# Gathered rows in a PEER layer: later picks behind every third block, and stores of a tile two pairs of blocks later

## The chip, the cores and the metric

One core of a Trainium2 chip runs the kernel. The metric is the device time of one execution in microseconds (us), the median of three runs; smaller is better. A profile comes from one further execution, which has its own time.

## The reference

Two decoder layers on 256 tokens of width 1024: a mixer (attention, then a convolution module), and after each mixer a PEER expert layer. The expert layer is what the change is about:

```python
u = expert_u[ec]                      # ec: 8 heads x 16 chosen experts of 16384 for each token
act = jax.nn.gelu(jnp.einsum('cd,chkd->chk', xc, u))
w = gc.astype(xc.dtype) * act
return jnp.einsum('chk,chkd->cd', w, expert_v[ec])
```

## The kernel before, in words

The kernel doesn't gather the rows of `expert_u`. In `peer` (L589) it goes through all 16384 experts in 128 blocks of 128, two blocks (a pair, `pi`) at a time: `s1_pair` (L162) multiplies a block of `u` with all 256 tokens, GELU is taken, and the result is multiplied by the gates of the tokens for these experts. Gates are mostly zero. They are made on TensorE in steps of 8 tokens while the pairs run (`gate_bank`), from pair 22 on; the first 128 tokens (a tile) have all their gates at pair 37, the second at pair 53 (`done`, the number of steps made, times `TB` = 8 tokens).

The second half of the layer multiplies the gated activations with the rows of `expert_v`. The last 32 blocks (`i` from 96 to 127) are taken as they lie: **the plain blocks**, 32 of them, each 12 matmuls of 128x512 (two tiles of tokens, two halves of the width, three terms of a split into high and low parts). Of the first 96 blocks only experts that some token uses are multiplied. For these, a table `expert` says which rows make up 84 new blocks of 128 rows, **the picked blocks**: 81 in the list `mixed` (42 that both tiles use, 12 matmuls each, and 39 that one tile uses, 6 matmuls; they alternate, both tiles first, and the last three are for both) and 3 in `ends`. The activations of the first 96 blocks are therefore written to a table `rows` in HBM, token columns by expert rows, with one DMA for 8 blocks and one tile (`send`, L627, on SP's queue).

Each picked block needs two indirect DMAs, both issued on POOL's queue:

- **a gather** (`picked`, L719): 128 rows of `expert_v`, 128x1024 f32, into one of four buffers `raw`. ACT casts it to `hi` (L122), DVE makes `lo` (L128), which frees the buffer, and TensorE multiplies (L146 to L148).
- **a pick** (`rows_of`, L726): the same 128 rows of `rows`, 128x256 f32, into one of 64 slots of `wr`. ACT casts it to `wh` (L731, in `row_parts`), DVE makes `wl` (L732). Slots are used again from the 65th pick on.

`pick` (L617) paces the picks: each has a dependence on the cast `wh` of the block that is being multiplied (`behind`). Once all 24 stores of `rows` are written into the program, two picks come behind each plain block, up to 64; then one comes behind each picked block until all 84 are made. A queue runs in order: a gather that stands behind a waiting pick waits too.

The order of instructions on each engine is not the program's. A scheduler places them by its own simulated times, so what the change moves is read from the built programs. At block `k` = 60 of `mixed` there is a conditional part (L697) that isn't taken with these inputs. Layer 0 and layer 1 of the PEER part are the same, except that layer 0's also prepares the convolution (`conv_prep`).

Of the kernel before, what the change touches and what calls it, by code (L numbers as in the profile page):

```python
# [15 lines left out]
P = 128  # L16
D = 1024
KC = D // P
T = 256
NT = T // P  # L20
# [17 lines left out]
HI = NK // 2  # L38
NC = 4 * TK + (TK - 4) * 4
TB = 8  # L40
# [5 lines left out]
NI = NK - ND  # L46
# [18 lines left out]
class Trunk:  # L65
# [523 lines left out]
    def peer(self, l, acc):  # L589
        nc, I = self.nc, self.I  # L590
        new = lambda: self.store_tile("st").rearrange("p (i t) -> p i t", t=T)
        st = [new()]
        sl = lambda i, n=2: st[i // HI][:, i % HI:i % HI + n, :]

        g = self.gain(2 * l + 1, st[0][:, HI - D // T:, :].rearrange("p i t -> p (i t)"))
        xT = self.norm_T(g, acc)
        U = I["u"][l]
        self.route_open(l)
        for h in range(PH):
            ps = self.s1_pair([I["wpq"][l, 2 * h], I["wpq"][l, 2 * h + 1]], xT, POOL_Q, h == 0)  # L600
            qT = self.qT[h % 2]
            nc.scalar.copy(qT, ps)
            self.route_scores(l, h, qT)
        route = self.route_steps()
        steps = 2 * (PH + 13)
        nb = T // TB
        done = 0
        rows = self.tc.dram_tile([NI * NK, T], F32, name=self.nm("rows"))
        out = rows.rearrange("(i j) t -> j i t", j=NK)
        sent = [0] * NT  # L610
        order = None
        mixed, ends = self.plan()
        turns = [b for _, b in mixed + ends]
        slot = lambda n: room[:, n % HI, :]
        picked = 0

        def pick(n, behind, most=HI):  # L617

            nonlocal picked
            for _ in range(min(n, min(most, len(turns)) - picked)):  # L620
                ins = self.rows_of(rows, turns[picked], slot(picked))
                self.tc.add_manual_dep(ins.ins, behind.ins.name,
                                       mybir.DependencyInfo(mybir.DependencyClass.Sync, mybir.DependencyReason.DATA),
                                       reason="pace")
                picked += 1

        def send(n, most):  # L627

            for t in range(NT):
                while most and done * TB >= (t + 1) * P and min(sent[t] + 8, NI) <= n and sent[t] < n:  # L630
                    i = sent[t]
                    m = min(8, n - i)
                    to = NT if t == 0 and sent[1] == i and done * TB >= T else t + 1
                    ts = slice(t * P, to * P)
                    nc.sync.dma_start(out[:, i:i + m, ts], sl(i, m)[:, :, ts])
                    for k in range(t, to):
                        sent[k] = i + m
                    most -= 1

        for pi in range(NK // 2):  # L640
            if pi == G0:
                for _ in route:
                    pass
                st.append(new())
                self.gates_open()
                self.one_hots(0)
                self.one_hots(1)
            due = min(max(0, pi + 1 - G0) * (nb // 2) // (G1 - G0), nb // 2) * 2
            todo = list(range(done, due))
            done = due  # L650
            if pi == G1:
                order = self.order_steps()

            def between(j):
                if j == 0:
                    for b in todo:
                        for q in range(TB // TQ):
                            self.gate_bank(b, q, 2 * pi, st)
                    if order is not None:
                        for _ in range(2):  # L660
                            next(order, None)

            ps = self.s1_pair([U[2 * pi], U[2 * pi + 1]], xT, between=between)
            for b in todo:
                if b + 2 < nb:
                    self.one_hots(b + 2)
            self.expert_rows(ps, sl(2 * pi), done * TB)
            if pi < G0:
                for _ in range((pi + 1) * steps // G0 - pi * steps // G0):
                    next(route, None)  # L670
            send(min(2 * pi - 2, NI), 1)
        for _ in order:
            pass

        room = self.store_tile("wr").rearrange("p (n t) -> p n t", t=T)
        acc = self.s2_open()
        self.begun = [[False] * 2 for _ in range(NT)]
        last = len(ends)
        for i in range(NI, NK):
            behind = self.expert_products(acc, self.weights(I["v%d" % l][i]), sl(i, 1)[:, 0, :], range(NT))  # L680
            send(NI, 1)
            if sent == [NI] * NT:
                pick(2, behind)
        prep = None
        for k, (ts, b) in enumerate(mixed):
            if k == 2:
                if l + 1 == DEPTH:
                    self.g_out = self.gain(2 * DEPTH, self.store_tile("g")[:, 0:D])
                else:
                    prep = self.conv_prep(l + 1)  # L690
            if prep is not None:
                next(prep, None)
            self.expert_products(acc, self.picked(l, b), slot(k), ts,
                                 0 in ts and not any(0 in v for v, _ in mixed[k + 1:]))
            pick(1, self.first_part, k + 1 + HI)
            if k == 3 * len(mixed) // 4:
                with self.tc.If(self.rest_needed > 0, preferred_fallthrough_block=False):  # L697
                    for b2 in range(NB):
                        ts2 = [t for t, (lo, hi) in enumerate(((0, A_END), (B_BEG, B_END))) if not lo <= b2 < hi]
                        if ts2:  # L700
                            w = self.wc.tile([P, T], F32, tag="wh", name=self.nm("wr"))
                            self.rows_of(rows, b2, w)
                            self.expert_products(acc, self.picked(l, b2), w, ts2)
        for _ in prep or ():
            pass
        ends = [(self.picked(l, b), self.row_parts(slot(len(mixed) + n), ts)) for n, (ts, b) in enumerate(ends)]
        prev = None
        for h in range(2):
            for n, (w, a) in enumerate(ends):
                mms = self.s2_mm(acc, w, a, 1, h, False, n == last - 1)  # L710
                if prev is not None:
                    self.after(mms[0], prev)
                prev = mms[-1]
        return acc
# [463 lines left out]
```

## Time and profile before

| | us |
|---|---|
| median of 3 runs | 1796.91 |
| lowest and highest | 1796.32, 1797.37 |
| the profiled execution's own time | 1814.46 |
| its span in the trace | 1812.7 |

| engine | busy us | share |
|---|---|---|
| TensorE, matmuls | 1735.5 | 96% |
| VectorE (DVE) | 1308.4 | 72% |
| ScalarE (ACT) | 913.4 | 50% |
| GpSimd (POOL) | 522.9 | 29% |

The span is the time between the first and the last instruction that the trace has. Matmuls are pipelined, so their busy time is no measure of how close TensorE is to its peak; the starts of the matmuls and of the work that feeds them say more. An indirect DMA shows on POOL with the time that POOL takes to issue it, not with the time of the transfer. The average over the whole span hides the stages: the two stretches of picked blocks, some 200 us each, have limits of their own.

### The profile page before, as it was taken

What the parts mean: (1) busy time and instruction counts of PE and PEld (TensorE: products, weight loads), DVE (VectorE), ACT (ScalarE), POOL (GpSimd) and SP (SyncE); (2) the same over time, 40 slices, a digit from 0 to 9 for tenths busy, and PEclk for the clock granted to TensorE, in tenths of its full rate; (3) what the DMA queues carried; (4) which work ended last, traced back from release to release, by engine and by line L of the source; (5) the groups of instructions that cost most, each with busy time, mean ns of one, the idle gap of its engine ahead of it and who ended that gap; (6) DMA issues with size and microseconds to landing.
All of it is one profiled execution on the core that took longest, in us unless ns stands there. A gap on an engine that the chain in (4) does not pass through costs nothing. (4 is left out here: it accounts for less than half of the span.)

```text
span 1812.7 us, 32893 instructions
## 1 busy us (share of the span) xinstructions
PE 1735.5 (96%) x12606; PEld 1580.6 (87%) x12606; DVE 1308.4 (72%) x2720; ACT 913.4 (50%) x1515; POOL 522.9 (29%) x447
## 2 busy tenths in 40 slices
PE   7999999999998998898999899999999999988988
PEld 6879999999998986677798799999999998866766
DVE  4667994787988655576788589947879886545656
ACT  4653455544443444676654534555444434445655
POOL 1304000000000577654376340000000006777543
PEclk9999999999999999899999899999999999999999
DMA  7435555447467777676742355554385677767765
GB/s 268 140 123 192 175 178 191 151 152 249 164 197 245 244 271 236 216 253 217 251 141 81 111 187 171 185 185 152 141 256 166 204 247 252 271 211 237 248 213 196
DMA packets 146284, 361.13 MB, mean 199 GB/s; under 512 B 13248, under 2 KB 64704, under 8 KB 146112
## 3 DMA queue, kind: packets, MB, share of 16 engines
q1 hardware_dynamic: 113856, 248.76, 40.6%
q0 software_dynamic: 32256, 110.12, 18.7%
q8 instruction: 103, 1.69, 0.4%
q14 instruction: 69, 0.57, 0.1%
HBM read 332.61 MB, written 26.21 MB: 198 GB/s over the span
## 5 line engine op out<-in xcount | busy, mean ns | idle before, releaser
L122 ACT CAST hi<-raw 128x1024 fp32r<-128x1024 f32 x576 | 602.9, 1048 | 611.5 <-PE ps_h L162 389.8
L128 DVE TENSOR_TENSOR lo<-raw,hi 128x1024 fp32r<-128x1024 f32 x530 | 647.2, 1222 | 315.7 <-ACT hi L122 287.1
L162 PE MATMUL ps_h<-xh,hi 128*128 128x256 f32 x2560 | 730.2, 286 | 2.3 <-ACT hi L122 2.3
L162 PE MATMUL ps_h<-xh,lo 128*128 128x256 f32 x2560 | 723.9, 284 | 4.7 <-DVE lo L128 4.6
L162 PE MATMUL ps_h<-xo,hi 128*128 128x256 f32 x2560 | 718.7, 284 | 0.0
L162 PEld LDWEIGHTS ps_h<-xh,lo 128*128 128x128 f32 x2560 | 491.7, 192 | 6.0 <-DVE lo L128 5.9
L162 PEld LDWEIGHTS ps_h<-xh,hi 128*128 128x128 f32 x2560 | 492.3, 192 | 4.6 <-ACT hi L122 2.5
L162 PEld LDWEIGHTS ps_h<-xo,hi 128*128 128x128 f32 x2560 | 488.5, 192 | 0.2
L726 POOL DMA_INDIRECT wr<-rows,expert x168 | 190.9, 1136 | 906.7 <-ACT ps_h L1078 843.2
L147 PE MATMUL acc<-lo,wh 128*128 128x512 f32 x760 | 305.3, 402 | 4.2 <-DVE lo L128 2.1
L148 PE MATMUL acc<-hi,wl 128*128 128x512 f32 x760 | 301.1, 396 | 0.0
L146 PE MATMUL acc<-hi,wh 128*128 128x512 f32 x760 | 222.9, 402 | 33.1 <-ACT hi L122 21.8
L719 POOL DMA_INDIRECT raw<-in_v_dram,expert x168 | 185.9, 1107 | 144.1 <-DVE wl L732 57.2
L146 PEld LDWEIGHTS acc<-hi,wh 128*128 128x128 f32 x760 | 143.0, 192 | 76.1 <-ACT hi L122 32.6
L147 PEld LDWEIGHTS acc<-lo,wh 128*128 128x128 f32 x760 | 145.8, 192 | 49.1 <-DVE lo L128 13.0
L148 PEld LDWEIGHTS acc<-hi,wl 128*128 128x128 f32 x760 | 145.8, 192 | 30.0
L128 POOL TENSOR_TENSOR lo<-raw,hi 128x1024 fp32r<-128x1024 f32 x46 | 109.5, 2385 | 137.5 <-ACT hi L122 124.2
L731 ACT CAST wh<-wr 128x256 fp32r<-128x256 f32 (+1 forms) x168 | 58.3, 349 | 62.1 <-PE acc L147 30.5
L1049 PE MATMUL ps_g<-oh 128*128 128x128 f16 x1024 | 87.0, 219 | 0.0
L1053 PE MATMUL uses<-oh 128*128 128x96 f16 x512 | 83.1, 204 | 0.0
L1066 DVE SCALAR_TENSOR_TENSOR st<-ps_g,st 128x256 f32<-128x256 f32 (+5 forms) x216 | 64.7, 334 | 24.1 <-PE ps_g L1049 24.1
L732 DVE TENSOR_TENSOR wl<-wr,wh 128x256 fp32r<-128x256 f32 (+1 forms) x168 | 59.1, 353 | 29.3 <-ACT wh L731 20.8
(210 smaller groups left out, 1509.4 us busy)
## 6 DMA issues: line engine op xcount, KB each, us to landing
raw<-in_u_dram SPq DMA_DIRECT2D x256, 512.0 KB
raw<-in_v_dram SPq DMA_DIRECT2D x64, 512.0 KB
rows<-st SPq DMA_DIRECT2D x48, 512.0 KB
raw<-in_wpq_dram SPq DMA_DIRECT2D x32, 512.0 KB
raw<-in_pw_dram SPq DMA_DIRECT2D x24, 512.0 KB
raw<-in_wqk_dram SPq DMA_DIRECT2D x16, 512.0 KB
raw<-in_wv_dram SPq DMA_DIRECT2D x8, 512.0 KB
raw<-in_wo_dram SPq DMA_DIRECT2D x8, 512.0 KB
```

The costliest lines, as they stand in the source:

```text
L122: ins = [nc.scalar.copy(hi, raw)]
L128: ins.append(eng.tensor_tensor(lo, raw, hi.bitcast(F32), op=ALU.subtract))
L146: return [mm(ps, wh, xh, start=first, stop=False), mm(ps, wh, xo, start=False, stop=False), mm(ps, wo, xh, start=False, stop=last)]
L147: mm(ps, wh, xo, start=False, stop=False),
L148: mm(ps, wo, xh, start=False, stop=last)]
L162: mm = self.nc.tensor.matmul(ps[:, j, :], w[:, c * P:(c + 1) * P], x[:, c, :], start=n == 0, stop=n == len(terms) - 1)
L719: self.nc.gpsimd.indirect_dma_start(raw, None, self.I["v%d" % l].rearrange("i j d -> (i j) d"), bass.IndirectOffsetOnAxis(ap=self.expert[: ...
L726: return self.nc.gpsimd.indirect_dma_start(w, None, rows, at)
L732: self.nc.vector.tensor_tensor(lo[:, cs], w[:, cs], hi[:, cs].bitcast(F32), op=ALU.subtract)
L1049: mm = nc.tensor.matmul(ps[:, t, :], self.oh[:, b % 2, 0, tp, :, e], self.oh[:, b % 2, 1 + k, tp, :, e], start=k == 0, stop=k == 1)
L1053: use = nc.tensor.matmul(self.uses[:, tok // P, :], self.oh[:, b % 2, 0, tp, :, e], self.oh[:, b % 2, 1, tp, 0:NI, e], start=tok == 0, sto ...
L1066: nc.vector.scalar_tensor_tensor(v, ps[:, :, lo:lo + m].rearrange("p t i -> p i t"), 1.0 / GS, v, op0=ALU.mult, op1=ALU.mult)
```

## The change

Two edits. In the loop over `mixed`, a pick comes behind every third block (`k % 3 == 0`) and not behind every block. And `send` goes by the gates that were done two pairs of blocks earlier (`past[-3]`), so that the program writes the stores of a tile two pairs later than it did.

```diff
         done = 0
+        past = [0] * 3
...
         def send(n, most):
+            summed = past[-3]
             for t in range(NT):
-                while most and done * TB >= (t + 1) * P and min(sent[t] + 8, NI) <= n and sent[t] < n:
+                while most and summed * TB >= (t + 1) * P and min(sent[t] + 8, NI) <= n and sent[t] < n:
...
-                    to = NT if t == 0 and sent[1] == i and done * TB >= T else t + 1
+                    to = NT if t == 0 and sent[1] == i and summed * TB >= T else t + 1
...
+            past.append(done)
             send(min(2 * pi - 2, NI), 1)
...
-            pick(1, self.first_part, k + 1 + HI)
+            if k % 3 == 0:
+                pick(1, self.first_part, k + 1 + HI)
```

Lines behind L630 have other numbers in the changed kernel: its gathers are L726, its picks L733, its casts `wh` L738.

SP's, ACT's and DVE's instructions stand in the same order in both programs, the 48 stores of `rows` among them; in TensorE's, two matmuls of one picked block have changed places. POOL's order has changed. The stores of the last groups of 8 blocks move from the plain block 96 to the plain blocks 96 to 98 in the program, so the two picks a block begin at plain block 98 and not at 96: 60 picks are made behind plain blocks, not 64, and 24 are left for the picked blocks, not 20. With one behind every third block, the last is made behind block 69.

POOL, layer 0, where the picked blocks begin (`wr` are picks, `raw` gathers, `conv` a memset of the convolution's buffers). Before:

```order
L726 DMA wr_7625<-rows_2057,expert 128x256 x60
L719 DMA raw_8399<-in_v_dram,expert 128x1024
L726 DMA wr_7625<-rows_2057,expert 128x256 x2
L719 DMA raw_8422<-in_v_dram,expert 128x1024
L726 DMA wr_7625<-rows_2057,expert 128x256 x2
L435 MEMSET conv_8439 128x1
L436 MEMSET conv_8439 128x8x30
L719 DMA raw_8444<-in_v_dram,expert 128x1024
L726 DMA wr_7625<-rows_2057,expert 128x256
L719 DMA raw_8468<-in_v_dram,expert 128x1024
L726 DMA wr_7625<-rows_2057,expert 128x256
L719 DMA raw_8486<-in_v_dram,expert 128x1024
```

The same place with the change:

```order
L733 DMA wr_7623<-rows_2057,expert 128x256 x56
L726 DMA raw_8395<-in_v_dram,expert 128x1024
L733 DMA wr_7623<-rows_2057,expert 128x256 x2
L726 DMA raw_8418<-in_v_dram,expert 128x1024
L733 DMA wr_7623<-rows_2057,expert 128x256 x2
L435 MEMSET conv_8434 128x1
L436 MEMSET conv_8434 128x8x30
L726 DMA raw_8439<-in_v_dram,expert 128x1024
L733 DMA wr_7623<-rows_2057,expert 128x256
L726 DMA raw_8462<-in_v_dram,expert 128x1024
L726 DMA raw_8480<-in_v_dram,expert 128x1024
L733 DMA wr_7623<-rows_2057,expert 128x256
```

Before, a pick stands between any two gathers from the third on, until the 23rd; now there is one for about three gathers, the last behind the 71st. In layer 1 two to four gathers stand between picks.

POOL, layer 0, where the gathers reach the conditional part. Before:

```order
L719 DMA raw_9582<-in_v_dram,expert 128x1024
L719 DMA raw_9605<-in_v_dram,expert 128x1024
L719 DMA raw_9622<-in_v_dram,expert 128x1024
L883 TENSOR_LOAD fitu
L697 COMPARE_AND_BRANCH
```

With the change:

```order
L726 DMA raw_9578<-in_v_dram,expert 128x1024
L733 DMA wr_7623<-rows_2057,expert 128x256
L726 DMA raw_9601<-in_v_dram,expert 128x1024
L726 DMA raw_9618<-in_v_dram,expert 128x1024
L733 DMA wr_7623<-rows_2057,expert 128x256
L890 TENSOR_LOAD fitu
L704 COMPARE_AND_BRANCH
```

Picks now stand among the gathers here, and one right ahead of the load that the branch goes by.

ACT in the changed program, the same order as before, in the middle of layer 0's picked blocks (`hi` is the cast of a gather, `wh` that of a pick's slot; `wh_9096` belongs to the block of `raw_9090`):

```order
L122 CAST hi_9051<-raw_9049 128x1024
L738 CAST wh_9096<-wr_7623 128x256
L444 ACTIVATE conv_8434<-ident,conv_8434 128x128
L122 CAST hi_9074<-raw_9072 128x1024
L738 CAST wh_9119<-wr_7623 128x128
L444 ACTIVATE conv_8434<-ident,conv_8434 128x128
L122 CAST hi_9092<-raw_9090 128x1024
```

Nothing moved here. The cast `wh` of a block stands right behind the cast `hi` of the block two earlier.

## Rows read from the trace of the kernel before

**Rows 1.** The page: span, and busy time, share of the span and instructions of each engine.
```profile
span 1812.7 us, 32893 instructions
...
PE 1735.5 (96%) x12606; PEld 1580.6 (87%) x12606; DVE 1308.4 (72%) x2720; ACT 913.4 (50%) x1515; POOL 522.9 (29%) x447
```

**Rows 2.** Stretches: us, busy of each engine, PE clock, DMA share, GB/s.
```profile
609.00:690.00 81.00, 79.50 (x347) 64.52 (x346) 46.74 (x58) 39.20 (x58) 58.80 (x55) 1.00 0.78 263
690.00:759.00 69.00, 59.28 (x218) 44.59 (x217) 32.51 (x45) 34.99 (x65) 51.50 (x49) 0.88 0.71 220
759.00:838.00 79.00, 78.38 (x334) 61.32 (x333) 55.65 (x75) 59.20 (x113) 43.21 (x39) 1.00 0.77 252
1592.00:1660.00 68.00, 57.73 (x225) 41.52 (x224) 34.90 (x47) 29.64 (x46) 53.68 (x47) 0.97 0.72 224
```

**Rows 3.** POOL in order of time, layer 0: start, duration, instruction, [idle before].
```profile
689.83 1.16 POOL L719 DMA_INDIRECT raw<-in_v_dram,expert  x1 [0.30 <-issue]
...
698.97 0.95 POOL L719 DMA_INDIRECT raw<-in_v_dram,expert  x1 [0.16 <-DMA wr<-rows,expert]
700.22 1.38 POOL L726 DMA_INDIRECT wr<-rows,expert  x1 [0.30 <-issue]
701.91 0.94 POOL L719 DMA_INDIRECT raw<-in_v_dram,expert  x1 [0.30 <-issue]
703.16 0.94 POOL L726 DMA_INDIRECT wr<-rows,expert  x1 [0.30 <-issue]
704.40 0.94 POOL L719 DMA_INDIRECT raw<-in_v_dram,expert  x1 [0.30 <-issue]
...
757.13 1.22 POOL L726 DMA_INDIRECT wr<-rows,expert  x1 [0.30 <-issue]
758.65 0.94 POOL L719 DMA_INDIRECT raw<-in_v_dram,expert  x1 [0.30 <-issue]
...
765.73 0.94 POOL L719 DMA_INDIRECT raw<-in_v_dram,expert  x1 [1.85 <-DMA raw<-in_v_dram,expert]
...
835.44 0.94 POOL L719 DMA_INDIRECT raw<-in_v_dram,expert  x1 [1.56 <-DVE wl L732]
837.41 0.94 POOL L719 DMA_INDIRECT raw<-in_v_dram,expert  x1 [1.03 <-DVE lo L128]
845.88 0.94 POOL L719 DMA_INDIRECT raw<-in_v_dram,expert  x1 [7.53 <-DVEq L697]
```

**Rows 4.** POOL in order of time, layer 1, three gathers.
```profile
1604.71 0.94 POOL L719 DMA_INDIRECT raw<-in_v_dram,expert  x1 [0.31 <-issue]
...
1666.06 0.93 POOL L719 DMA_INDIRECT raw<-in_v_dram,expert  x1 [1.46 <-DVE lo L128]
...
1736.90 0.94 POOL L719 DMA_INDIRECT raw<-in_v_dram,expert  x1 [1.88 <-DVE wl L732]
```

**Rows 5.** POOL groups, 701.9 to 759, then 765 to 838: busy, mean ns | idle.
```profile
L726 POOL DMA_INDIRECT wr<-rows,expert x19 | 21.8, 1147 | 8.6 <-issue 5.2 <-DVE wl L732 3.1 <-DVE lo L128 0.3
L719 POOL DMA_INDIRECT raw<-in_v_dram,expert x20 | 20.7, 1034 | 6.9 <-issue 5.5 <-DVE wl L732 1.4
...
L719 POOL DMA_INDIRECT raw<-in_v_dram,expert x35 | 40.1, 1146 | 34.4 <-DVE wl L732 16.0 <-DVE lo L128 11.7 <-DMA raw<-in_v_dram,expert 3.9
```

**Rows 6.** Waits, 690 to 760, then 765 to 838: total us, times, longest.
```profile
ACT hi L122 <- DMA raw<-in_v_dram,expert: 17.2, 11, 3.3
...
POOL raw L719 <- DVE wl L732: 16.0, 13, 1.7
ACT hi L122 <- DMA raw<-in_v_dram,expert: 12.1, 17, 1.2
```

**Rows 7.** ACT, then POOL, in order of time, plain blocks of layer 0.
```profile
614.14 0.41 ACT L731 CAST wh<-st 128x256 fp32r<-128x256 f32 x1 [1.36 <-PE acc L147]
...
616.86 0.41 ACT L731 CAST wh<-st 128x256 fp32r<-128x256 f32 x1 [1.36 <-PE acc L147]
...
612.09 0.94 POOL L726 DMA_INDIRECT wr<-rows,expert  x1 [1.82 <-ACT wh L731]
```

## The prediction

> **What bounds the kernel now.** The page first, for the size: a span of 1812.7 us, TensorE's matmuls busy in 96% of it, POOL in 29% [rows 1]. By these shares a change to POOL's queue is worth nothing. But they are averages, so I read the stages next. In the plain blocks (609 to 690) and in the picked blocks from 759 on, TensorE is busy nearly throughout. In the first picked blocks it isn't: 59.28 of 69 us in layer 0 and 57.73 of 68 in layer 1, where the DMA engines move 220 to 224 GB/s against 263 in the plain blocks and 252 later [rows 2]. So data come late there, though the DMA engines have room.
>
> Third, POOL in order of time. From the fourth gather at 701.91 to the 23rd at 758.65, picks and gathers take turns, and nearly each starts 0.30 us behind the one before, released by nothing but "issue" [rows 3]. A pick takes 1147 ns and a gather 1034 ns of POOL in that stretch, so a block needs at least 1.147 + 1.034 + 2 x 0.30 = 2.78 us. The rows give (758.65 - 701.91) / 19 = 2.99 us. Picks end at 757.13. From the 27th gather (765.73) to the 60th (835.44) a block takes 69.71 / 33 = 2.11 us [rows 3], in layer 1 (1736.90 - 1666.06) / 33 = 2.15 [rows 4]. Mean: 2.13 us. POOL is idle for 34.4 us before those 35 gathers and waits for DVE, that is, for a free buffer [rows 5]. Fourth, the waits agree: ACT waits 17.2 us for gathered data in the early stretch, 11 times, 3.3 us at worst; later 12.1 us, 17 times and 1.2 at worst, and POOL's waits for DVE come first [rows 6].
>
> So **POOL's issuing sets the pace of the first 23 picked blocks of each layer**. What is then the floor of TensorE? A plain block of 12 matmuls takes 616.86 - 614.14 = 2.72 us [rows 7]. Picked blocks have 12 or 6, 9 in the mean, so 2.04 us. At 2.13 the gather-only stretch is near it.
>
> **The stores, two pairs later.** SP's order is the same in both programs, so this edit moves no store. What it does: 60 picks are made behind plain blocks, not 64. The four that drop out are the first ones, for blocks 96 and 97. Would that bring the first gather forward? No: the ninth pick, at 612.09, waited 1.82 us for ACT's cast [rows 7], so the queue has no backlog there to lose, and from then on the picks wait for the same casts as before. I cost it at nothing and keep the first four gathers (689.83 to 701.91) as they are, with the third one late at 698.97 [rows 3]. If that cover is gone, four issues of 1.45 us a layer come off.
>
> **The picks behind every third block.** Three gathers and a pick take POOL 3 x (1.034 + 0.30) + 1.147 + 0.30 = 5.45 us, 1.82 a block [rows 5]. That is below 2.13, so POOL no longer sets the pace. The new pace is 2.13 plus x, where x is a third of what one pick costs in a stretch that was free of picks. The trace has no such stretch, so I bound a pick:
> - from below by nothing. POOL has 34.4 / 35 - 0.30 = 0.68 us a block to spare there, 2.05 in three blocks, more than the pick's 1.45.
> - by data: a pick moves 128x256 numbers, a quarter of a gather's 128x1024. Were the DMA engines the limit, it would cost a quarter of 2.13, 0.53 us. Their share is 0.77 [rows 2], so they are not quite that.
> - from above by the whole of POOL's 1.45 us, if it always stands just ahead of a gather whose buffer is free.
>
> I take 0.25 us, about half of the data price, since POOL's spare time covers its issue: x = 0.08, a pace of 2.21.
>
> Does a pick now hold up the gathers behind it? It waits for the cast `wh` of its block, and ACT makes this right behind the cast `hi` of the block two earlier. The gather ahead of the pick in the queue needs the buffer of just that earlier block, which DVE frees only after that `hi`. So by the time POOL reaches the pick, its wait is over. The pick ahead of the branch (block 60) is covered too: POOL's next gather stands 7.53 us there, for DVE's sequencer [rows 3].
>
> **The sum**, against the profiled execution:
> - Fourth to 27th gather, 23 blocks: 765.73 - 701.91 = 63.82 us in layer 0, 1666.06 - 1604.71 = 61.35 in layer 1 [rows 3, 4]. At 2.13 both would take 49.0, which saves 14.8 + 12.4 = 27.2 us.
> - At the start of it buffers are free, so three gathers can go at POOL's pace of 1.82 and not 2.13: 3 x 0.31 x 2 = 1.9 us.
> - x is paid in 23 blocks there and in 43 further ones up to block 69, twice: 132 x 0.08 = 10.6 us.
>
> 27.2 + 1.9 - 10.6 = **18.5 us** less. The granted clock of 0.88 in the early stretch, a part of it at the lower of the two levels (1.2 and 2.4 GHz) behind gaps of TensorE [rows 2], is contained in the 63.82 and isn't counted again. The profiled execution took 1814.46 us, 17.55 more than the median of 1796.91; no view says where that lies, so I carry the difference over: 1796.9 - 18.5 = **1778.4 us**. With x from 0 to 0.18 (the data price) the gain is 29.1 to 5.3, so 1768 to 1792. If the stretch came down to TensorE's 2.04, 46 blocks gain a further 4.1: 1764.
>
> A rule speaks against this. The Trainium skill (DMA: Bandwidth & Descriptors, section "Anatomy of one DMA") says that making descriptors is a small part of such a DMA's time and that its fixed cost of about 2 us is the wait for completion, not the setup. By it the sum of the issues isn't what paces the gathers, a pick costs about its bytes wherever it stands, and the change is worth nothing. The trace disagrees: POOL is taken for more than 1 us an issue, back to back [rows 3, 5].
>
> **The rivals.** The bound for a difference is 0.2%, 3.6 us: about what a measurement of this kernel can tell from no change.
> - *A pick costs the same wherever it stands.* In the early stretch 19 picks a layer came with 27.2 us of delay, 27.2 / 38 = 0.72 us each. If that is data and not issuing, x is 0.24 and the change gives 29.1 - 31.7: 2.6 us slower, 1799.5. For it: ACT waits for data in both stretches [rows 6]. Against it: 220 GB/s in the stretch with picks, 263 in the plain blocks [rows 2]. By the section of the Trainium skill named above (DMA: Bandwidth & Descriptors) it would go this way.
> - *The late picks become the pace* (slower). The gather-only stretch is a loop through four buffers that is released by DVE [rows 6]. A pick that comes just ahead of a released gather delays it by up to 1.45 us, and the loop doesn't get that back. It decides from 0.66 us a pick on (29.1 / 132 = 0.22 a block). At 1.0 us: 132 x 0.33 = 43.6, so 14.5 us slower, 1811.4; at 1.45, 1831. Against it: the spare 2.05 us in three blocks.
> - *Nothing of it is the picks'.* If the third gather's lateness at 698.97 goes as well and TensorE runs at 2.04 from the start, the gain passes 33 us, below 1764. Against it: the queue ahead of that gather is as long as before.
>
> **How the numbers follow.** Forecast (x up to 0.18): 0.75. Same price: 0.12. Late picks as the pace: 0.07. The larger gain: 0.06. The range leaves out the last two and the worse half of the same price, 0.19 together: 1764 to 1795. Faster: 0.75 + 0.06, less 0.01 for a gain that just misses the bound, 0.80. Same: that 0.01 and 0.10 of the same price, 0.11. Slower: the late picks' 0.07 and 0.02 of the same price, 0.09.
>
> **What would show it.** Right: in the early stretch POOL waits for DVE and not for "issue", gathers from the eighth on come every 2.1 to 2.3 us, DMA moves about 250 GB/s, TensorE's granted clock is near 1.00 there, and from 765 on a block takes 2.2. The stores stand where they stood, and the ninth pick's time is unchanged. Wrong: gathers stay 2.7 us or more apart although picks are fewer (data, not issuing); or blocks 26 to 69 take over 2.35 us with POOL waiting at picks for ACT; or the first gathers have moved.

## The result

The changed kernel takes 1782.55 us (median of 4 runs, 1781.04 to 1786.41); the kernel before, beside it, 1797.14 (4 runs, 1796.32 to 1799.82). Ratio 0.9921, 95% interval 0.9905 to 0.9938: 14.6 us faster, where 18.5 were forecast. It is inside the range.

The profiled execution of the change took 1786.41 us. That is 28 us below the profiled one of before (1814.46), twice the difference of the medians. About half of this isn't the change's: it stands in the plain blocks, which neither edit shortens (the table under "The first gathers").

**The profile after.** The page: span, then the engines, to be held against [rows 1].

```profile
span 1784.6 us, 32897 instructions
...
PE 1721.6 (96%) x12606; PEld 1576.6 (88%) x12606; DVE 1309.7 (73%) x2720; ACT 913.8 (51%) x1515; POOL 527.3 (30%) x447
```

The shares have hardly moved. The work is the same; only its places are other ones.

Stretches of the change, columns as in [rows 2]: plain blocks, then gathers 1 to 27, then 27 to 60 of layer 0, then 1 to 27 of layer 1.

```profile
609.00:683.00 74.00, 74.00 (x328) 61.30 (x327) 45.15 (x55) 37.56 (x56) 55.19 (x53) 1.00 0.84 282
683.00:745.00 62.00, 61.58 (x268) 49.61 (x267) 40.95 (x54) 41.79 (x78) 45.58 (x42) 1.00 0.79 254
745.00:818.00 73.00, 71.01 (x292) 52.91 (x291) 48.18 (x65) 52.24 (x99) 51.88 (x44) 1.00 0.79 257
1572.40:1633.70 61.30, 59.92 (x260) 48.05 (x259) 39.46 (x52) 34.07 (x53) 45.54 (x38) 1.00 0.77 246
```

In the early stretch of layer 0 TensorE is busy in 61.58 of 62 us, and its granted clock is 1.00, where before it was 59.28 of 69 at 0.88 [rows 2]. The DMA engines move 254 GB/s there, not 220. In the next stretch TensorE lost a little: 71.01 of 73 us, where before it was busy in 78.38 of 79 [rows 2].

POOL of the change in order of time, layer 0: start, duration, instruction, [idle before]. Gathers are now L726, picks L733.

```profile
611.83 1.00 POOL L733 DMA_INDIRECT wr<-rows,expert  x1 [7.58 <-ACT wh L738]
...
682.90 0.96 POOL L726 DMA_INDIRECT raw<-in_v_dram,expert  x1 [0.30 <-DVE wl L739]
...
693.77 0.94 POOL L726 DMA_INDIRECT raw<-in_v_dram,expert  x1 [0.30 <-issue]
695.02 1.46 POOL L726 DMA_INDIRECT raw<-in_v_dram,expert  x1 [0.30 <-issue]
696.78 0.95 POOL L733 DMA_INDIRECT wr<-rows,expert  x1 [0.30 <-issue]
698.04 1.35 POOL L726 DMA_INDIRECT raw<-in_v_dram,expert  x1 [0.30 <-issue]
699.69 0.93 POOL L726 DMA_INDIRECT raw<-in_v_dram,expert  x1 [0.30 <-issue]
701.52 0.94 POOL L726 DMA_INDIRECT raw<-in_v_dram,expert  x1 [0.90 <-DVE wl L739]
...
734.87 0.94 POOL L726 DMA_INDIRECT raw<-in_v_dram,expert  x1 [1.39 <-DVE lo L128]
736.11 1.06 POOL L733 DMA_INDIRECT wr<-rows,expert  x1 [0.30 <-issue]
737.48 1.67 POOL L726 DMA_INDIRECT raw<-in_v_dram,expert  x1 [0.30 <-issue]
...
744.69 1.06 POOL L726 DMA_INDIRECT raw<-in_v_dram,expert  x1 [0.30 <-issue]
...
816.73 1.06 POOL L733 DMA_INDIRECT wr<-rows,expert  x1 [0.30 <-issue]
818.10 1.59 POOL L726 DMA_INDIRECT raw<-in_v_dram,expert  x1 [0.30 <-issue]
```

The rows shown are the first pick behind plain block 100 (611.83), the first gather (682.90), the fourth (693.77) to the eighth (701.52), the 23rd (734.87), the 27th (744.69) and the 60th (818.10). Up to the seventh gather POOL issues back to back, and the buffers fill. At the eighth it waits for DVE. From there to the 23rd a block takes (734.87 - 701.52) / 15 = 2.22 us, where it was 2.99. From the 27th to the 60th it takes (818.10 - 744.69) / 33 = 2.22, where it was 2.11 [rows 3].

Layer 1 of the change, the fourth, 27th and 60th gather:

```profile
1583.24 0.94 POOL L726 DMA_INDIRECT raw<-in_v_dram,expert  x1 [0.30 <-issue]
...
1633.74 0.93 POOL L726 DMA_INDIRECT raw<-in_v_dram,expert  x1 [0.64 <-DVE lo L128]
...
1707.49 1.50 POOL L726 DMA_INDIRECT raw<-in_v_dram,expert  x1 [0.30 <-issue]
```

POOL's groups of the change, 693.7 to 735, then 744.6 to 818.2, columns as in [rows 5]:

```profile
L726 POOL DMA_INDIRECT raw<-in_v_dram,expert x20 | 22.2, 1112 | 10.1 <-DVE wl L739 4.0 <-issue 4.0 <-DVE lo L128 2.2
L733 POOL DMA_INDIRECT wr<-rows,expert x6 | 7.5, 1248 | 2.5 <-ACT conv L444 1.3 <-issue 0.9 <-ACT hi L122 0.3
...
L726 POOL DMA_INDIRECT raw<-in_v_dram,expert x34 | 39.1, 1149 | 17.3 <-DVE wl L739 7.2 <-issue 6.7 <-DVE lo L128 3.4
L733 POOL DMA_INDIRECT wr<-rows,expert x11 | 14.7, 1339 | 4.2 <-ACT wh L738 2.1 <-issue 0.9 <-ACT conv L444 0.6
```

Between the 20 gathers there were 19 picks; now there are six, and more of POOL's idle time before a gather is a wait for DVE (6.2 us) than issue (4.0). In the later stretch POOL's idle time before gathers fell from 34.4 us [rows 5] to 17.3, since 11 picks stand there now. With 1339 ns a pick is dearer than the 1147 it was.

Waits of the change, 683 to 745, then 744 to 818.2: total us, times, longest.

```profile
ACT hi L122 <- DMA raw<-in_v_dram,expert: 9.6, 14, 1.4
...
ACT hi L122 <- DMA raw<-in_v_dram,expert: 16.2, 18, 1.7
POOL raw L726 <- DVE wl L739: 7.2, 8, 1.4
PEld acc L147 <- DVE lo L128: 6.8, 14, 0.7
POOL raw L726 <- issue: 6.7, 22, 0.3
...
POOL wr L733 <- ACT wh L738: 2.1, 4, 0.7
```

ACT's waits for gathered data fell in the early stretch from 17.2 us (3.3 at worst) to 9.6 (1.4), and rose in the later one from 12.1 us to 16.2 [rows 6]. A part of the delay has moved behind the early stretch.

### The profile page after: what moved, and what is told of

The parts are those of the page before. It is cut to its first block, busy times and chain, and to the rows that moved or that the text cites. A ratio compares the mean times of both kernels' runs of the same rounds, so it can differ in the third digit from the quotient of the medians.

```text
span 1784.6 us, 32897 instructions
## 1 busy us (share of the span) xinstructions
PE 1721.6 (96%) x12606; PEld 1576.6 (88%) x12606; DVE 1309.7 (73%) x2720; ACT 913.8 (51%) x1515; POOL 527.3 (30%) x447
## 5 line engine op out<-in xcount | busy, mean ns | idle before, releaser
L733 POOL DMA_INDIRECT wr<-rows,expert x168 | 187.9, 1118 | 912.4 <-ACT ps_h L1085 842.4
L147 PE MATMUL acc<-lo,wh 128*128 128x512 f32 x760 | 300.7, 396 | 4.2 <-DVE lo L128 3.0
L146 PE MATMUL acc<-hi,wh 128*128 128x512 f32 x760 | 218.4, 396 | 20.0 <-ACT hi L122 13.2
L726 POOL DMA_INDIRECT raw<-in_v_dram,expert x168 | 193.3, 1151 | 104.8 <-issue 35.5
L146 PEld LDWEIGHTS acc<-hi,wh 128*128 128x128 f32 x760 | 142.3, 190 | 57.7 <-ACT hi L122 21.0
L738 ACT CAST wh<-wr 128x256 fp32r<-128x256 f32 (+1 forms) x168 | 58.3, 348 | 45.5 <-PE acc L147 36.9
L1076 ACT ACTIVATE st<-ps_g 128x256 f32<-128x256 f32 (+16 forms) x168 | 42.5, 305 | 68.8 <-DVE st L1073 61.1
```

The costliest lines, as they stand in the source:

```text
L146: return [mm(ps, wh, xh, start=first, stop=False), mm(ps, wh, xo, start=False, stop=False), mm(ps, wo, xh, start=False, stop=last)]
L147: mm(ps, wh, xo, start=False, stop=False),
L726: self.nc.gpsimd.indirect_dma_start(raw, None, self.I["v%d" % l].rearrange("i j d -> (i j) d"), bass.IndirectOffsetOnAxis(ap=self.expert[: ...
L733: return self.nc.gpsimd.indirect_dma_start(w, None, rows, at)
L738: self.first_part = self.nc.scalar.copy(hi[:, cs], w[:, cs])
```

## The experiments

The theory: POOL's issuing of two indirect DMAs a block paces the first 23 picked blocks, and a pick taken out of that pace costs little elsewhere. The main rival: a pick costs its data, wherever it stands. Then: which of the two edits gives what. Twelve runs were made, in three sets (e1 to e4, e5 to e8, e9 to e12), each on a chip of its own. The kernel before, run beside them each time, took 1821.56, 1820.76 and 1795.40 us. So ratios are compared across sets, and microseconds only within one.

| kernel | us | the kernel before beside it | ratio, 95% interval |
|---|---|---|---|
| e1_before_again | 1822.76 | 1821.56 | 1.0002 (0.9980 to 1.0025) |
| e2_third_only | 1802.17 | 1821.56 | 0.9895 (0.9864 to 0.9926) |
| e3_stores_only | 1828.10 | 1821.56 | 1.0034 (1.0013 to 1.0055) |
| e4_no_late | 1784.70 | 1821.56 | 0.9792 (0.9753 to 0.9831) |
| e5_after_again | 1808.70 | 1820.76 | 0.9905 (0.9875 to 0.9936) |
| e6_third_again | 1798.70 | 1820.76 | 0.9856 (0.9831 to 0.9882) |
| e7_narrow | 1820.70 | 1820.76 | 0.9991 (0.9971 to 1.0010) |
| e8_by_sp | 1787.23 | 1820.76 | 0.9816 (0.9783 to 0.9849) |
| e9_after_third_time | 1783.40 | 1795.40 | 0.9939 (0.9918 to 0.9960) |
| e10_third_third_time | 1779.31 | 1795.40 | 0.9920 (0.9899 to 0.9942) |
| e11_less_four | 1783.28 | 1795.40 | 0.9930 (0.9905 to 0.9956) |
| e12_fourth | 1783.47 | 1795.40 | 0.9928 (0.9908 to 0.9948) |

### The kernel before once more

No edit.

> The kernel before, unchanged: a second profiled execution of it, and a ratio that must be 1. Theory A (the first profiled execution was a disturbed one: 1814.46 us against a median of 1797): this profile takes about 1800 us, ACT's casts of the plain blocks come every 2.72 us without gaps of 4 to 5 us, and the first gather of layer 0 stands near 683 us, where the changed kernel has it, not at 690. Theory B (being profiled slows a stretch that POOL's issuing paces): the profile again takes about 1814 us and the first gather stands near 690. Under both, gathers and picks take turns at 2.7 to 3.0 us a block from the 4th gather to the 23rd.

1822.76 us, ratio 1.0002. On this chip the same program takes 1.4% longer than the 1796.91 shown before the prediction. Neither theory fits. The profiled execution took 1825.55 us, with the first gather of layer 0 at 690.43, so it isn't the quick one that theory A wanted; and it isn't slower than its kind, as theory B has it, since the other nine took 1816.55 to 1829.55. From the fourth gather to the 23rd a block takes 3.05 us in layer 0 and 2.98 in layer 1.

### Picks behind every third block, stores as before

```diff
-            pick(1, self.first_part, k + 1 + HI)
+            if k % 3 == 0:
+                pick(1, self.first_part, k + 1 + HI)
```

> Only the first edit: a late pick behind every third block, stores as before, so 64 picks behind plain blocks and 20 late ones. Theory A (the picks' spacing is the whole gain): 1778 to 1783 us, as the changed kernel or up to 3 us better, since 4 late picks a layer are fewer; first gather where the kernel before has it. Rival (the later stores give part of the gain by taking four picks from the head of POOL's queue, so that the first gather comes earlier): 1785 to 1793 us.

1802.17 us, 19.4 less than before. The expected microseconds were meant for the chip of the first comparison; the ratio of 0.9895 would be 1778 us there, at the lower end of theory A's range. The first gather stands at 691.03, near that of the kernel before. The first edit alone gives at least what the whole change does. Run again on a second chip:

> The third-block edit alone, again, to stand beside the changed kernel on one chip. Theory A: ratio 0.987 to 0.991, 2 to 5 us below the changed kernel. Rival (the later stores help): above the changed kernel.

1798.70 us, 22.1 less than before, and 10.0 less than the whole change beside it (e5). The ratio, 0.9856, is just below theory A's range, and the distance to the whole change is twice the 5 us at the upper end of what it said.

### Stores two pairs later, picks behind every block

```diff
+            summed = past[-3]
...
+            past.append(done)
```

> Only the second edit: stores two pairs later, so 60 picks behind plain blocks, and 24 late ones behind every block. Theory A: no gain; 8 more late picks at up to 0.7 us each, 1797 to 1803 us. Rival (four picks fewer at the head of POOL's queue bring the first gather forward): 1784 to 1793 us.

1828.10 us, 6.5 more than before: the stores edit alone makes the kernel slower. It turns four early picks a layer into late ones, eight in all; 6.5 / 8 = 0.8 us each (0.3 to 1.25 by the interval), about what a late pick costs in the kernel before (next).

### No late picks at all

```diff
-            pick(1, self.first_part, k + 1 + HI)
```

The 20 late picks of each layer are left out, so the last 20 picked blocks are multiplied with old slots.

> The kernel before without the 20 late picks of each layer: the last 20 picked blocks multiply by the activations of other blocks, so this part of the computation is wrong data, at the same amount of work. It is the floor of what moving late picks can give. Theory A (POOL's issuing paces the early stretch, and in the changed kernel 24 late picks a layer still cost about 0.3 us each): all gathers come every 2.1 us, and the time is 10 to 15 us below the changed kernel, about 1770. Rival (a pick costs the same wherever it stands, 0.7 us): the floor is 40 x 0.7 = 28 us below the kernel before, about 1769, and the changed kernel would not have gained from it. Third (late picks cost the changed kernel nothing): the same time as the changed kernel, 1782.

1784.70 us. The 40 late picks cost (1821.56 - 1784.70) / 40 = 0.92 us each behind every block; behind every third one, by e2, (1802.17 - 1784.70) / 40 = 0.44. POOL without them, from the fourth gather to the 23rd (700.5 to 740):

```profile
L718 POOL DMA_INDIRECT raw<-in_v_dram,expert x19 | 21.1, 1108 | 18.6 <-DVE wl L731 10.3 <-DVE lo L128 4.6 <-DMA raw<-in_v_dram,expert 2.5
```

No idle time goes to issue among the larger parts; DVE's release of a buffer sets the pace, as it did in the gather-only stretch [rows 5]. A block takes (740.18 - 700.54) / 19 = 2.09 us, as theory A had it. Its price of 0.3 us for a late pick of the changed kernel looks too low: by the ratios this kernel lies 0.0129 below the changed one, 23 us of 1797 and not 10 to 15. The two other theories fall, since the changed kernel gained and its late picks do cost something.

### Late picks with an eighth of the bytes

```diff
+                if picked < HI:
                     ins = self.rows_of(rows, turns[picked], slot(picked))
+                else:
+                    ins = self.rows_of(rows.rearrange("n (a b) -> (n a) b", b=32), turns[picked], slot(picked)[:, 0:32])
```

Late picks fetch 32 numbers a row, not 256; the rest of their slots keeps what stood there.

> The kernel before with each late pick narrowed to 32 of 256 numbers a row: an eighth of the bytes, the same number of issues, the same order (the late slots hold wrong activations). Theory A (what a late pick costs is POOL's issue): 0.995 to 1.000 of the kernel before, gathers still 2.7 to 3.0 us apart in the early stretch. Rival (it is the bytes): most of what leaving the late picks out gave, ratio 0.980 to 0.985, gathers 2.2 us apart.

1820.70 us, ratio 0.9991: seven eighths of their bytes are gone, and so is nothing of the time. POOL's groups of this kernel, 701.6 to 757.6:

```profile
L729 POOL DMA_INDIRECT wr<-rows,expert x19 | 22.4, 1176 | 6.2 <-issue 6.2
L722 POOL DMA_INDIRECT raw<-in_v_dram,expert x19 | 20.5, 1079 | 7.0 <-issue 5.2 <-DVE lo L128 1.5 <-DVE wl L735 0.3
```

A pick of 16 KB takes POOL 1176 ns, one of 128 KB 1147 [rows 5]. The picture of the queue is that of before, issue after issue, and a block takes (757.64 - 701.60) / 19 = 2.95 us; only the order differs a little, since some picks now stand in pairs with two gathers behind them.

### Late picks with the same bytes, issued on SP's queue

```diff
+                if picked < HI:
                     ins = self.rows_of(rows, turns[picked], slot(picked))
+                else:
+                    ins = nc.sync.dma_start(slot(picked), rows[picked * NK:(picked + 1) * NK, :])
```

Late picks are plain DMAs of 128 rows that lie together, so they fetch other rows than the reference's.

> The kernel before with each late pick made by a plain DMA of the same 128x256 numbers from SP's queue at the same point (rows in their order, so the late slots hold wrong activations): the same bytes at the same places in time, no issue on POOL. Theory A (issue): ratio 0.980 to 0.985, near the kernel without late picks, gathers about 2.2 us apart from the 4th on. Rival (bytes): 0.997 to 1.000, gathers 2.7 to 3.0 us apart.

1787.23 us, ratio 0.9816 (0.9783 to 0.9849); without late picks it was 0.9792 (0.9753 to 0.9831). The bytes are all there, POOL's 40 issues are not, and the gain is about that of leaving the picks out. The stretch 690 to 750 of this kernel, columns as in [rows 2]:

```profile
690.00:750.00 60.00, 58.47 (x247) 45.19 (x246) 38.78 (x53) 39.40 (x74) 34.98 (x33) 1.00 0.86 286
```

286 GB/s: the DMA engines had room for the picks all along. The gathers come (741.63 - 700.70) / 19 = 2.15 us apart, and what ends POOL's idle time before them is mostly DVE or an earlier gather, not issue. POOL's group of this kernel, 702 to 757:

```profile
L722 POOL DMA_INDIRECT raw<-in_v_dram,expert x26 | 31.0, 1193 | 25.5 <-DVE wl L735 12.3 <-DMA raw<-in_v_dram,expert 6.0 <-DVE lo L128 4.2
```

With e7 this separates the issue from the bytes. Two things changed at once here, the queue and which rows are fetched; a pick of scattered rows from another queue wasn't tried, nor what in an indirect DMA takes POOL its microsecond.

### The whole change again, and what the stores edit costs in it

> The changed kernel again, beside its two single edits on one chip. The chip of the first four runs took 1821 us for the kernel before, where the chip of the first comparison took 1797, so ratios are compared. Theory A (spacing gives the gain; the later stores only turn 4 early picks a layer into late ones): ratio 0.990 to 0.994, 2 to 5 us slower than the third-block edit alone, and the first gather stands where it does in the other kernels of this call. Rival (the two edits help each other: the first gather 7 us earlier, as in the changed kernel's first profile): ratio 0.985 or less, below the third-block edit alone, first gather 7 us earlier than in the others.

1808.70 us, 12.1 less than before, with the first gather of layer 0 where the others of this set have it, and not at 682.90:

```profile
690.61 0.96 POOL L726 DMA_INDIRECT raw<-in_v_dram,expert  x1 [0.30 <-issue]
```

The ratio is theory A's, and the rival falls. The distance to the first edit alone is 10.0 us, not 2 to 5.

The last set has the whole change, the first edit alone, and two new kernels side by side.

> The whole change once more, as the measure for the three kernels beside it. Both theories: ratio to the kernel before 0.988 to 0.994. First gather of layer 0 about 690 and 60 picks ahead of the sixth gather's stretch (56 before the first gather), 24 behind picked blocks in each layer.

> Picks behind every third block, stores as in the kernel before (64 picks behind plain blocks, 20 behind picked ones in each layer). If each late pick at its new place costs about 0.45 us, this has 8 late picks fewer than the whole change and is 3 to 6 us faster than it: ratio to the kernel before 0.985 to 0.990, 0.002 to 0.004 below the whole change. If the stores edit is free, as the prediction had it, the two have the same ratio within 0.001.

In e11 the last four picks of a layer, which the stores edit had made late ones, are left out; in e12 the stores are as before.

```diff
-            if k % 3 == 0:
+            if k % 3 == 0 and picked < len(turns) - 4:
```

> The whole change with the last four picks of each layer left out (80 picks, 60 of them behind plain blocks and 20 behind picked ones; the last four blocks are multiplied with what an earlier block left in their slots). Theory A, the stores edit costs only because it turns four picks a layer into late ones: the ratio is that of the third-block kernel beside it, within 0.002, and 0.002 to 0.005 below the whole change. Theory B, the stores edit costs by another way (the stores' own time, the slots, the first gathers): the ratio stays within 0.001 of the whole change.

```diff
-            if k % 3 == 0:
+            if k % 4 == 0:
```

> Picks behind every fourth block, stores as in the kernel before: the same 20 late picks a layer, spread from the first to the 77th block instead of to the 58th. Theory A, every late pick in a stretch paced by DVE costs the same 0.45 us: the ratio equals that of the third-block kernel within 0.002, and the cadence of gathers 1 to 23 is about 2.36 against 2.45, that of 62 to 84 about 0.1 higher. Theory C, a pick costs less the more time lies between two: 40 picks at about 0.3 us, 6 us and 0.003 below the third-block kernel. If the last picks come too late for their blocks, TensorE waits for DMA wr in the last blocks and the ratio is above that of the third-block kernel.

The whole change takes 1783.40, inside its range, but with the first gather of layer 0 at 683.00 and not at 690. The first edit alone takes 1779.31: 4.1 us less again, though the two intervals overlap, and with 0.9920 above its range of 0.985 to 0.990. Leaving the eight picks out (e11) gives 1783.28, 0.1 us, where theory A wanted some 4; but the intervals of e9, e10 and e11 all overlap, so this set doesn't tell A from B. Nor do the traces. From the first gather to the last, layer 0 takes 191.2 us in e9, 189.1 in e10 and 189.0 in e11, as A has it; layer 1 takes 191.5, 190.8 and 193.3, which it doesn't explain.

Every fourth block (1783.47) is no better than every third: theory C falls. A late pick isn't made cheaper by spreading it further than that.

## Why the prediction was right, and where its sum was off

**POOL's issuing set the pace.** Right. Narrow picks changed nothing, and picks moved off POOL gave nearly all of what leaving them out gives. The Trainium skill (DMA: Bandwidth & Descriptors, section "Anatomy of one DMA"), by which making descriptors is a small part of a DMA's time, doesn't carry over to what paces this queue: e7 and e8 disagree with it, with the ratios 0.9991 and 0.9816. The rival "a pick costs the same wherever it stands" falls with it: 0.92 us a pick behind every block, 0.44 behind every third.

**The early stretch.** Fourth to 27th gather: 744.69 - 693.77 = 50.9 us and 1633.74 - 1583.24 = 50.5, where they were 63.82 and 61.35 [rows 3, 4]. That is 23.8 us less; the terms of the prediction for this stretch, 27.2 + 1.9 - 46 x 0.08, gave 25.4. What it said would be seen is there: waits for DVE from the eighth gather on, 2.22 us a block, 254 GB/s, a clock of 1.00. The lower clock in the early stretch went with the gaps, as the prediction treated it: 0.88 with TensorE busy in 59.28 of 69 us [rows 2], 1.00 with 61.58 of 62.

That the size came out so near is in part luck. The prediction had one profile of the kernel before, and this stretch isn't as steady as one profile makes it look: in e1, the same kernel, it takes 69.00 and 66.34 us, and the change in e5, on another chip with equally long plain blocks, 51.85 and 51.33. Between these two it is 32.2 us.

**The price of a late pick: the term that was mis-sized.** The prediction took 0.25 us for a pick in a stretch paced by DVE, "since POOL's spare time covers its issue". Between the 27th and the 60th gather the change takes 73.41 and 73.75 us where 69.71 and 70.84 were taken [rows 3, 4]: 6.6 us more, 0.30 a pick, and the prediction had 66 x 0.08 = 5.3. From the 60th gather to the last it takes a further 3.7 us, where 1.6 were forecast; but e4, which has no late picks, takes as long there as the change (57.5 and 57.7 us, against 58.4 and 56.4), so this part isn't shown to be the picks'.

The best pair is e2 and e4, on one chip. The medians give 0.44 us a pick, uncertain by some 0.2. The traces give 0.36: from the fourth gather to the 60th, both layers, e2 takes 248.6 us and e4 235.0, with 38 picks between. (e6 against e8 gives (1798.70 - 1787.23) / 40 = 0.29, but there the picks' data still come, by another queue, so that is a part of the price.) All lie above 0.25, if not clear of it, and below the 0.66 from which the change would have been slower.

The spare time of POOL is real, but it isn't where the pick needs it: in the rows at 736.11 and 816.73 a pick is issued just before a gather, and the gather then starts with "issue" as its releaser and not DVE. The pick's own wait for ACT, which the prediction had as over by then, is small but not gone: 2.1 us ahead of four of the 11 picks between the 27th and the 60th gather.

**The stores: not free.** Against the first edit alone the whole change is 10.0 us slower in one set and 4.1 in another; alone the stores edit costs 6.5. The prediction costed this edit at nothing for the first gathers. The four further late picks a layer are in its sum, since x is paid up to block 69, but at 0.25 us they are only 8 x 0.25 = 2 us; at 0.29 to 0.44 they are 2 to 4. That it is these picks and nothing else isn't shown, since e11, which leaves them out, came out at the whole change's time. A part of the 10.0 us may not be the edit's: in the profile of e5 16.4 us pass from the last gather of layer 0 to the last product, in that of e6 11.2, and kernels without the stores edit have such a late end too (16.3 in e2, 14.5 in e7). What else the edit costs stays open. So the sum is: first edit 16.1 to 22.1 us less in the three sets, second edit 4 to 10 us back, together 12.0 to 14.6, where 18.5 were forecast.

**The first gathers.** "Wrong: the first gathers have moved", said the prediction, and in the profile after they had: 682.90 for 689.83. That goes with the chip and not with the edits. The time from the first product of a plain block to the first gather, and from there to the last product, in eight of the fourteen profiles (us, layer 0 and layer 1; starts of POOL's first gather, start of the first and end of the last matmul into `acc`):

| profile | the kernel before beside it | plain blocks | picked blocks |
|---|---|---|---|
| before | | 81.1, 81.5 | 212.1, 212.8 |
| e1_before_again | 1821.56 | 80.7, 82.0 | 218.2, 216.9 |
| e5_after_again | 1820.76 | 81.1, 81.6 | 213.0, 205.6 |
| e6_third_again | 1820.76 | 81.3, 81.5 | 205.8, 203.7 |
| e8_by_sp | 1820.76 | 82.1, 82.1 | 197.0, 194.0 |
| after | 1797.14 | 74.5, 74.5 | 206.3, 204.6 |
| e9_after_third_time | 1795.40 | 74.5, 74.5 | 205.9, 203.3 |
| e10_third_third_time | 1795.40 | 74.5, 74.5 | 201.2, 202.1 |

The other six agree: 80.3 to 82.1 us of plain blocks in e2, e3, e4 and e7, 74.5 in e11 and e12. The same program, the change, has 81 us in the set of e5 and 74.5 in its first profile and in that of e9, and within a set the edits make no difference. So of the 28 us between the two profiled executions, (81.1 + 81.5) - 2 x 74.5 = 13.6 belong to the chip, and the picked blocks give 14.0, near the 14.6 of the medians. By parts, both layers, these 14.0 are 23.8 less from the fourth gather to the 27th and 2.8 less ahead of it, then 6.6 more up to the 60th, 3.7 more up to the last, and 2.2 more behind it. The table also suggests where much of the 17.55 us lies that the prediction carried over without a place. Which chips the first two profiles came from isn't on record, and a profile of the kernel before with the short plain blocks wasn't taken, so that last point rests on the other kernels.

**The plain picks.** Right: the pick behind plain block 100 stands at 611.83, where it was 612.09 as the ninth [rows 7]. It is now the fifth, and waited 7.58 us.

**A version that beats both.** Picks behind every third block with the stores left as they were: 1798.70 against 1808.70 (the change) and 1820.76 (before), and 1779.31 against 1783.40 and 1795.40, where the intervals of the first two overlap.

## What to carry to other kernels

When a queue's rows stand back to back with "issue" as releaser, add up its issues per block before looking at bytes; an issue moved to another queue, or to a stretch with another pace, is worth its time down to what paces the stretch next: here (1820.76 - 1787.23) / 40 = 0.84 us (e8) of the 1.45 that a pick took POOL, since DVE's release of buffers then sets 2.1 us a block. At the new place it isn't free just because that engine is idle on the mean: about half of what a late pick cost came back here (0.44 of 0.92 us), where some are issued just ahead of a gather whose buffer is free. And before two profiles are subtracted, compare a stage that the change doesn't touch: if it differs, the edit isn't the only difference between them.

## What was not expected of the hardware

The chips differ: one program took 1795.40 to 1821.56 us in the median on four occasions, 1.5%. For the change, 1808.70 and 1783.40 us in e5 and e9, about half of the difference stands in the plain blocks (table above). There ACT's casts follow each other every 2.72 us on a faster chip and stop at times on a slower one. ACT in order of time, e9 and then e1 (plain blocks of layer 0):

```profile
627.58 0.41 ACT L738 CAST wh<-st 128x256 fp32r<-128x256 f32 x1 [1.36 <-PE acc L147]
630.30 0.41 ACT L738 CAST wh<-st 128x256 fp32r<-128x256 f32 x1 [1.36 <-PE acc L147]
```

```profile
626.33 0.41 ACT L731 CAST wh<-st 128x256 fp32r<-128x256 f32 x1 [1.63 <-PE acc L148]
630.66 0.41 ACT L731 CAST wh<-st 128x256 fp32r<-128x256 f32 x1 [2.98 <-remote]
```

In e1, from 609 to 683, ACT waits 13.6 us in four such places ("remote", a releaser that the trace doesn't name); in e9 there is none. What is late there wasn't tried.

And an indirect DMA's time on POOL hardly depends on its bytes: 1176 ns for 16 KB, 1147 for 128 KB, 1034 to 1149 for 512 KB ([rows 5] and the groups of the change).
